# FoX's forget sums of the next head pair, issued from ScalarE's queue

## The chip, the cores and the metric

The kernel runs on 1 core of one Trainium2 chip. The metric is the device time of one execution in microseconds (us), as the median of several runs. The engines are named as in the profile: PE (TensorE's matmuls), PEld (its weight loads), DVE (VectorE), ACT (ScalarE), POOL (GpSimd), SP (SyncE, which here only issues DMAs). A q behind a name (SPq, ACTq) means that engine's sequencer: its queue, in which DMA issues and waits stand.

## The reference

One layer of a decoder trunk with 2048 tokens of 1024 channels in float32. What matters here is the forgetting attention (FoX) with 8 heads of 64 channels. Eight stick-breaking heads precede it, and the output projection, a gated MLP and a final norm follow it.

```
F = cumsum(log_f)                            # per head, over the 2048 tokens
s = q_blk . k * HEAD_DIM**-0.5               # one block of 128 queries
s = s + F_blk[..., None] - F[:, None, :]     # the forget sums
s = where(kpos <= qpos, s, -inf)
p = softmax(s)
out = p . v
```

F at the query's own position shifts a whole row and drops out of the softmax, so a kernel needs only F at the key positions, the same 2048 numbers for every query of a head.

## The kernel before

The attention runs over 32 units (kind, p, tb): first the stick-breaking heads ("sb"), then FoX ("fox"), each with four pairs p of heads, and for each pair four blocks tb of 512 queries. A unit handles two sub-blocks `j2` of 256 queries, and in each the two heads `hl` of the pair. The work grows with tb, since query block tb attends to all keys up to its own; the last block of a pair, tb = 3, is the longest, and the first block of the next pair, tb = 0, the shortest.

`fox_head` computes one head for 256 queries, as two rows of tiles (`qi`) of 128 queries. For each chunk of up to 512 keys, two matmuls (L596, L597) make the negated logits in PSUM; DVE (L675) adds the forget sums `Fb[ch]` and keeps the running minimum `mn`. For the chunk on the diagonal GpSimd (L672) first makes a masked copy `Fd` of the sums. ScalarE then takes the exponential of the whole row at once (L679), up to 2048 wide. After both rows, `weighted` transposes the probabilities on PE (L606), copies them out of PSUM as a high and a low half `at` (ScalarE L610, DVE L611) and multiplies them with V (L615).

`load_sums(p)` loads the forget sums of a pair: four tiles `Fb` of 128 x 1024 (512 KB each), for two heads and two halves of the keys, each a row of the DRAM tensor `fs` broadcast to all partitions (L653). They share four buffers (tag "xt"), so the next pair's sums can only be loaded when the old ones have been read for the last time, in unit tb = 3, `j2` = 1. `load_sums` is called at the start of unit tb = 0 of a pair (for pair 0 in unit 14, long before), and issues on SyncE's queue.

On the same queue go, among others, the loads of Q, K and V of the next unit (`load_unit`, L362 to L364), the loads `hp<-hs` of the projections' operands (`proj`, L468), those of the late modulation (`late_mod`, L776), `gate_m` (L796) and the stores of results. The projections of later units (`proj`, matmuls at L342 and L413) are interleaved with the attention: `follow` pulls them along by the goals of `pace`. What order the instructions take in each engine's queue is planned when the program is built, by a simulation of time; `tc.issue_after(ins)` forces what is written inside it to stand behind `ins` in the queue of that engine. The plan also lets every DMA, from whichever of the two queues, signal one of eight semaphores in turn.

Of the kernel before, what the change touches and what calls it, by code (L numbers as in the profile page):

```python
# [9 lines left out]
F32 = mybir.dt.float32  # L10
F32R = mybir.dt.float32r
BF16 = mybir.dt.bfloat16
AF = mybir.ActivationFunctionType
# [4 lines left out]
P = 128  # L18
S = 2048
D = 1024  # L20
# [4 lines left out]
TB = 512  # L25
NTB = S // TB
# [8 lines left out]
def kernel(ctx: ExitStack, tc: tile.TileContext, x, c, w_ada, b_ada, g_attn, w_in, b_fgate,  # L35
                      g_out_fox, g_out_sb, w_out, g_mlp, w_up, conv_w, conv_b, w_down, g_final, out):
    nc = tc.nc
# [30 lines left out]
    fs = dram.tile([NH, S], F32, name="fs")  # L68
# [56 lines left out]
    def open_pool(name, side=None, space=None):  # L125
        st = pools[name] = ExitStack()
        kw = dict(space=space) if space is not None else {}
        return st.enter_context(tc.tile_pool(name=name, bufs=1, side=side, reuse_waits="tile", **kw))
# [9 lines left out]
    px = open_pool("px", side="right")  # L138
    sm = open_pool("mod", side="right")

    def bank(pool, tag, bufs):
        return pool.tile([P, 512], F32, name=f"ps_{tag}", tag=tag, bufs=bufs)
# [74 lines left out]
    b = pv()  # L217
# [376 lines left out]
    def logits(cw, qcols, hl, Q, K):  # L594
        b = qk()
        nc.tensor.matmul(b[:, :cw], Q[:, hl, 0, qcols], K[:, hl, :cw], start=True, stop=False)  # L596
        marks.append(nc.tensor.matmul(b[:, :cw], Q[:, hl, 1, qcols], K[:, hl, :cw], start=False, stop=True).ins)  # L597
        return b
# [46 lines left out]
                         ch == n - 1 and m == 0, ch == 0 and m == nk - 2, kts[0] == 2 * j)  # L645
                yield

    def load_sums(p):
        sums = [[], []]
        for t in range(0, NTB, 2):  # L650
            for h in range(2):
                b = px.tile([P, D], F32, name="Fb", tag="xt", bufs=4)
                nc.sync.dma_start(b, fs[2 * p + h:2 * p + h + 1, t * TB:(t + 2) * TB].to_broadcast([P, D]))  # L653
                sums[h] += [b[:, 0:TB], b[:, TB:D]]
        return sums

    def fox_head(j, qc, hl, Q, K, V, o, Fb, ls):
        n = (2 * j + 2 + 3) // 4
        rows_ = []
        for qi in range(2):  # L660
            W = (2 * j + qi + 1) * P
            a = sx.tile([P, S], F32, name="p", bufs=4)
            mn = None
            for ch in range(n):
                need = min(512, W - ch * 512)
                b = logits(max(need, 2 * P), slice((qc + qi) * P, (qc + qi + 1) * P), hl, Q, K[ch])
                sl = slice(ch * 512, ch * 512 + need)
                m2 = sx.tile([P, 1], F32, name="mn", bufs=8)
                add = Fb[ch]
                if ch == n - 1:  # L670
                    add = px.tile([P, TB], F32, name="Fd", tag="hf_a", bufs=2)
                    mask[:] = [nc.gpsimd.affine_select(  # L672
                        out=add[:, :need], in_=Fb[ch][:, :need], pattern=[[-1, need]], base=need - P,
                        channel_multiplier=1, compare_op=ALU.is_ge, fill=BIG).ins]
                nc.vector.tensor_tensor_reduce(out=a[:, sl], in0=b[:, :need], in1=add[:, :need], scale=1.0,  # L675
                                               scalar=3e38 if mn is None else mn, op0=ALU.add, op1=ALU.min,
                                               accum_out=m2)
                mn = m2
            nc.scalar.activation(a[:, 0:W], a[:, 0:W], AF.Exp, scale=-1.0, bias=mn, accum_out=ls[:, hl, qc + qi:qc + qi + 1])  # L679
            rows_.append(a)  # L680
            yield
        for m in range(0, 2 * j + 2, 2):
            weighted(o, [m, m + 1], lambda kt, qi: rows_[qi][:, kt * P:(kt + 1) * P], V, hl, m == 0, m == 2 * j,
                     m == 2 * j)
            yield

    sums, step, mask = [], [], []
    deferred = []
    marks = []

    def tick(n=1):
# [5 lines left out]
    def attend(kind, p, tb, res, Fbs):  # L697
        Q = res[tb][0]
        K = [r[1] for r in res]
        V = [r[2] for r in res]  # L700
        oT = sb.tile([P, TB], F32, name="oT", bufs=2)
        last_unit = (kind, p, tb) == units[-1]
        if kind == "fox":
            ls = sx.tile([P, 2, 4], F32, name="ls", bufs=2)
        mp = p if kind == "fox" else p + 4

        def head_var(j2):
            sq = (sx.tile([P, 2 * P], F32, name="sq", bufs=1) if kind == "sb" and (p, tb) != (3, NTB - 1) else
                  px.tile([P, TB], F32, name="sq", tag="z", bufs=2)[:, 0:2 * P])
            cols_ = slice(j2 * 2 * P, (j2 + 1) * 2 * P)  # L710
            nc.gpsimd.tensor_mul(sq, oT[:, cols_], oT[:, cols_])

            def reduce():
                b = bank(psd, "t", 2) if last_unit and j2 else pt()
                for t in range(2):
                    nc.tensor.matmul(b[:, 2 * t:2 * t + 2], sq[:, t * P:(t + 1) * P], headsel, start=True, stop=True)
                v = var[tb][:, 2 * j2:2 * j2 + 2, 2 * mp:2 * mp + 2]
                bv = b[:, 0:4].rearrange("p (t h) -> p t h", t=2)
                if kind == "fox":
                    l = ls[:, :, 2 * j2:2 * j2 + 2]  # L720
                    nc.vector.scalar_tensor_tensor(l, l, EPS, l, ALU.mult, ALU.mult)
                    nc.vector.scalar_tensor_tensor(v, bv, 1.0 / HD, l.rearrange("p h t -> p t h"), ALU.mult, ALU.add)
                else:
                    nc.vector.tensor_scalar(v, bv, 1.0 / HD, EPS, ALU.mult, ALU.add)

            deferred.append([reduce, 13])

        for j2 in range(2):
            j = 2 * tb + j2
            for hl in range(2):  # L730
                o = bank(psc, "bc", 2) if (kind, p, tb) == units[-2] else pv()
                if kind == "sb":
                    yield from sb_head(j, 2 * j2, hl, Q, K, V, o)
                else:
                    yield from fox_head(j, 2 * j2, hl, Q, K, V, o, Fbs[hl], ls)
                o2 = sb.tile([HD, 2 * P], F32, name="o2", bufs=2)
                step[1] = nc.scalar.activation(o2, o[HD:P, 0:2 * P], AF.Copy).ins
                nc.vector.tensor_add(oT[hl * HD:(hl + 1) * HD, j2 * 2 * P:(j2 + 1) * 2 * P], o[0:HD, 0:2 * P], o2)
            head_var(j2)
        nc.sync.dma_start(os_[mp][tb], oT)  # L740
        yield
# [285 lines left out]
    Fbs = None  # L1027
    tail = None
    big = orp = None
    for i, u in enumerate(units):  # L1030
        kind, p, tb = u
        nxt = units[i + 1] if i + 1 < len(units) else None
        if u == ("sb", 1, 0):
            forget_sums()
            next(lm)
        if u == ("fox", 0, 0):
            close_pool("sx")
            sx = open_pool("fx", side="right")
        if i == 14 or (kind == "fox" and tb == 0 and p):
            Fbs = load_sums(p if kind == "fox" else 0)  # L1040
        n = attend_steps(u)
        if i >= len(units) - 2:
            head_root(i - len(units) + 2)
            head_scale(i - len(units) + 2, pt(), sx)
        if nxt is None:
            tail = first_out()
        if i == len(units) - 2:
            for _ in ahead:
                projected[0] += 1
            drain(lm)  # L1050
            close_pool("sl", "psa")
            psc = open_pool("psc", side="right", space=PSUM)
            big = open_pool("big")
            orp = open_pool("orp")
            tail = first_mix()
        goals = list(pace(i))

        def follow(m):
            while projected[0] < goals[min(m, n - 1)]:
                with tc.issue_after(marks[max(0, len(marks) - 1 - LAG)]) if START <= i < ENDQ else nullcontext():  # L1060
                    if next(ahead, 1) is not None:
                        break
            if nxt and projected[1] > i + 1 and loaded_units[0] == i + 1:
                loaded_units[0] += 1
                load_unit(*nxt, results[nxt[:2]])

        interleave(attend(kind, p, tb, results[kind, p], Fbs), n, [(lm if i >= LATE else None, PER, False), (tail, 17 + IDLE if nxt is None else 13, True)], follow)
        while nxt and loaded_units[0] == i + 1:
            next(ahead, None)
            follow(n)  # L1070
# [225 lines left out]
    for u in range(1, NU):  # L1296
        for c in range(8 if u == 1 else 0, 16):
            t, n, q = chunk(u, c)
# [148 lines left out]
    for sblk, order in enumerate(orders):  # L1447
# [47 lines left out]
        a, b = bank_a(), bank_a()  # L1495
# [32 lines left out]
    for kp in range(PRE):  # L1528
        if kp % 2 == 0:
            pre = ho.tile([P, 2, 2, TB], F32, name="pre", tag="xh", bufs=3)  # L1530
        t = pre[:, kp % 2]
# [153 lines left out]
    for i in range(7):  # L1685
        nxt = {}
        kept = []
        for s in range(2):
# [7 lines left out]
            for kp in range(NKP):  # L1696
                a = ahead_a.pop((i, s, kp), None)
                if a is None:
                    a = a_operand(i, s, kp, raw_a())
# [63 lines left out]
```

## Time and profile before

| What | Value |
|---|---|
| median of 3 runs | 2949.75 us (2949.39 to 2951.26) |
| the profiled execution's own time | 2943.39 us |
| its span | 2941.4 us |
| mean granted TensorE clock | 0.993 |
| busy: PE, PEld, DVE, ACT, POOL | 97%, 84%, 74%, 57%, 31% |
| DMA | 601.89 MB, mean 205 GB/s |
| loads of the forget sums (L653) | 16 of 512 KB, all on SyncE |

The span is the time from the first to the last instruction of the one profiled execution; the execution's own time is 2.0 us longer. Times in the views count from the span's start. In a timeline each row has start, duration, engine, line and tiles, and, in brackets, how long the engine sat idle before and who ended that. In a list of waits each row has who waited, for whom, the total, how often and the longest. In a table of stretches each row has the stretch, its length, the busy time and number of instructions of PE, PEld, DVE, ACT and POOL, the granted clock, the share of the DMA engines and GB/s.

### The profile page before, as it was taken

To read this page: it belongs to the slowest core of one execution; us is meant where nothing else is said; L and a number is where in the kernel's file an instruction comes from. 1 tells how busy PE (TensorE), PEld (TensorE's weight loads), DVE (VectorE), ACT (ScalarE), POOL (GpSimd) and SP (SyncE) were. 2 spreads that over 40 slices of the span, in tenths; PEclk is the share of its full clock that TensorE was granted. 3 is DMA by queue.
4 is the path that set the end of the run, shared out by engine and by line. 5 is a ranking of instruction groups with operands and counts; after the bars stand their busy time and mean duration, and the time that the engine had idled before them with its cause. 6 is when DMAs were issued, how large, how long until landed. Compare 5 with 4: busy or idle time off the path is not lost.

```text
span 2941.4 us, 45922 instructions
## 1 busy us (share of the span) xinstructions
PE 2867.8 (97%) x15772; PEld 2459.7 (84%) x15772; DVE 2179.5 (74%) x3464; ACT 1686.0 (57%) x3187; POOL 901.1 (31%) x967
## 2 busy tenths in 40 slices
PE   8999999999999999999999999999999999999998
PEld 7888888888988988888888788888788888888887
DVE  5787778877886656658843788888998888575476
ACT  5776767677776656658744554444444445433342
POOL 0431322243032423231213344444254543142200
PEclk8999999999999999999999999999999999999999
DMA  9749756867469794794537775554754444975644
GB/s 293 255 139 321 236 188 207 301 211 229 162 212 356 269 277 139 232 323 140 182 120 233 245 232 128 130 136 129 236 132 125 130 130 132 309 257 185 216 158 151
DMA packets 348346, 601.89 MB, mean 205 GB/s; under 512 B 34672, under 2 KB 178800, under 8 KB 348112
## 3 DMA queue, kind: packets, MB, share of 16 engines
q1 hardware_dynamic: 324208, 558.06, 57.7%
q0 software_dynamic: 10880, 20.97, 4.3%
q10 hardware_dynamic: 13024, 19.93, 1.9%
q8 instruction: 124, 2.03, 0.3%
q14 instruction: 110, 0.90, 0.1%
HBM read 420.77 MB, written 177.02 MB: 203 GB/s over the span
## 4 chain that ended last, share of the span: by engine, by line
PE 46%; DMA 3%; DVE 2%; SPq 1%; ACT 1%; issue 1%; POOL 0%; DVEq 0%; ACTq 0%; POOLq 0%
PE ps_o L1315 19%; PE ps_t L1315 7%; PE ps_o L1614 6%; PE ps_t L1614 3%; PE ps_bc L1614 3%; PE ps_o L912 1%; PE ps_pv L615 1%; DMA r<-rstd 1%; PE ps_bc L912 1%; PE ps_pt L606 1%; PE ps_o L1609 1%; DMA wo<-wos 1%; DMA hm<-hf_m 1%; SPq L895 1%; DVE op L46 1%
## 5 line engine op out<-in xcount | busy, mean ns | idle before, releaser
L1315 PE MATMUL ps_o<-op,wu 128*128 128x512 f32 x2592 | 608.0, 389 | 2.0 <-DVE snap L1366 1.5
L1315 PEld LDWEIGHTS ps_o<-op,wu 128*128 128x128 f32 x2592 | 486.2, 188 | 103.9 <-DVE snap L1366 1.9
L611 DVE TENSOR_TENSOR at<-ps_pt,at 128x512 fp32r<-128x512 f32 (+1 forms) x576 | 366.1, 652 | 100.2 <-ACT at L610 97.3
L636 DVE TENSOR_TENSOR_SCAN a<-r,a 128x512 f32<-128x512 f32 (+2 forms) x320 | 368.3, 1167 | 77.8 <-ACT a L631 39.9
L342 PE MATMUL ps_pj<-hp,w_qk 128*128 128x512 f32 x1512 | 411.2, 403 | 14.5 <-DMA hp<-hs 12.9
L610 ACT ACTIVATE at<-ps_pt 128x512 fp32r<-128x512 f32 (+1 forms) x576 | 318.5, 576 | 139.1 <-PE ps_pt L606 123.1
L615 PE MATMUL ps_pv<-at,V 128*128 128x256 f32 x2216 | 386.8, 292 | 9.3 <-DVE at L611 4.2
L615 PEld LDWEIGHTS ps_pv<-at,V 128*128 128x128 f32 x2216 | 320.9, 190 | 39.8 <-DVE at L611 11.4
L342 PEld LDWEIGHTS ps_pj<-hp,w_qk 128*128 128x128 f32 x1512 | 275.4, 190 | 71.0 <-DMA hp<-hs 16.2
L45 ACT ACTIVATE wu<-wuraw 128x512 fp32r<-128x512 f32 x204 | 128.9, 632 | 248.5 <-PE ps_o L1315 190.1
L596 PE MATMUL ps_qk<-K,Q 128*128 128x512 f32 (+2 forms) x640 | 265.7, 416 | 5.6 <-ACT a L631 3.3
L413 PE MATMUL ps_pj<-w_v,hp 128*128 128x256 f32 (+1 forms) x1536 | 236.6, 288 | 2.1 <-DVE hp L422 1.6
L597 PE MATMUL ps_qk<-K,Q 128*128 128x512 f32 (+2 forms) x640 | 235.7, 369 | 0.0
L1315 PE MATMUL ps_t<-op,wu 128*128 128x512 f32 x888 | 220.8, 390 | 1.0 <-DVE op L46 1.0
L413 PEld LDWEIGHTS ps_pj<-w_v,hp 128*128 128x128 f32 x1536 | 209.0, 189 | 10.9 <-DVE q L373 1.5
L630 ACT ACTIVATE r<-ps_qk 128x512 f32<-128x512 f32 (+2 forms) x320 | 173.1, 541 | 58.2 <-PE ps_qk L597 55.5
L46 DVE TENSOR_TENSOR wu<-wuraw,wu 128x512 fp32r<-128x512 f32 x204 | 189.6, 930 | 18.1 <-ACT wu L45 16.7
L1315 PEld LDWEIGHTS ps_t<-op,wu 128*128 128x128 f32 x888 | 166.4, 188 | 36.5 <-DVE op L46 1.8
L606 PE MATMUL ps_pt<-edge,a 128*128 128x128 f32 x1088 | 185.1, 274 | 8.4 <-DVE a L636 7.8
L1614 PE MATMUL ps_o<-op 128*128 128x512 f32 x840 | 191.5, 389 | 0.0
L1614 PEld LDWEIGHTS ps_o<-op 128*128 128x128 f32 x840 | 157.7, 188 | 32.7
L679 ACT ACTIVATE p<-p,mn 128x128 f32<-128x128 f32 (+15 forms) x128 | 153.9, 1203 | 53.3 <-DVE mn L675 52.2
(342 smaller groups left out, 5237.6 us busy)
## 6 DMA issues: line engine op xcount, KB each, us to landing
hp<-hs SPq DMA_DIRECT2D x224, 512.0 KB
wuraw<-in_w_up_dram SPq DMA_DIRECT2D x80, 512.0 KB
ra<-g SPq DMA_DIRECT2D x136, 256.0 KB
rb<-in_w_down_dram SPq DMA_DIRECT2D x108, 256.0 KB
g<-u SPq DMA_DIRECT2D x80, 256.0 KB
hs<-hp SPq DMA_DIRECT2D x32, 512.0 KB
hp<-in_w_ada_dram SPq DMA_DIRECT2D x32, 512.0 KB
qk_fox<-q SPq DMA_DIRECT2D x32, 512.0 KB
```

Source lines behind the costliest of these rows:

```text
L46: (lo_engine or nc.gpsimd).tensor_sub(lo, src, f(hi))
L342: nc.tensor.matmul(acc, w[kt][:, a, n], h[:, bb], start=kt == 0 and i == 0, stop=kt == KT - 1 and i == 2)
L413: nc.tensor.matmul(av[:, t * width:(t + 1) * width], hts[kt][:, a, tok], w[1][kt][:, bb, 0:width], start=kt == 0 and m == 0, stop=kt == KT ...
L596: nc.tensor.matmul(b[:, :cw], Q[:, hl, 0, qcols], K[:, hl, :cw], start=True, stop=False)
L597: marks.append(nc.tensor.matmul(b[:, :cw], Q[:, hl, 1, qcols], K[:, hl, :cw], start=False, stop=True).ins)
L606: nc.tensor.transpose(b[:, i * P:(i + 1) * P], blk(kts[kk], qi), ident)
L610: copies = [nc.scalar.activation(at[:, 0, lo:], b[:, lo:], AF.Copy).ins, nc.vector.tensor_sub(at[:, 1, lo:], b[:, lo:], f(at[:, 0, lo:])).ins]
L611: nc.vector.tensor_sub(at[:, 1, lo:], b[:, lo:], f(at[:, 0, lo:])).ins]
L615: m = nc.tensor.matmul(o[:, 0:2 * P], V[kt // 4][:, kt % 4, hl, :], rhs, start=first and kk == 0 and w == 0, stop=last and kk == 1 and w == 1)
L636: nc.vector.tensor_tensor_scan(rev, r[:, 0:need][:, ::-1], rev, 0.0 if right[qi] is None else right[qi][:, 0:1], ALU.mult, ALU.add)
L1315: nc.tensor.matmul(b, w[:, p, j], o[:, q], start=first and i == 0, stop=last and i == 2, skip_group_check=True)
L1614: nc.tensor.matmul(b, a[:, p, t * P:(t + 1) * P], w[:, q], start=first and i == 0, stop=last and i == 2, skip_group_check=True)
```

## The change

`load_sums` now loads one head's two tiles, on a queue that it is given. For pairs 1 to 3 it is no longer called at the start of the pair. Instead it is called from within `fox_head` of the pair before, in unit tb = 3, `j2` = 1: once for each head, behind the exponential of the head's last row, on ScalarE's queue. Pair 0's sums stay in unit 14 on SyncE, now head by head.

```diff
-    def load_sums(p):
-        sums = [[], []]
+    def load_sums(p, hl, queue=nc.sync):
+        sums = []
         for t in range(0, NTB, 2):
-            for h in range(2):
-                b = px.tile([P, D], F32, name="Fb", tag="xt", bufs=4)
-                nc.sync.dma_start(b, fs[2 * p + h:2 * p + h + 1, t * TB:(t + 2) * TB].to_broadcast([P, D]))
-                sums[h] += [b[:, 0:TB], b[:, TB:D]]
+            b = px.tile([P, D], F32, name="Fb", tag="xt", bufs=4)
+            queue.dma_start(b, fs[2 * p + hl:2 * p + hl + 1, t * TB:(t + 2) * TB].to_broadcast([P, D]))
+            sums += [b[:, 0:TB], b[:, TB:D]]
         return sums
...
-            nc.scalar.activation(a[:, 0:W], a[:, 0:W], AF.Exp, scale=-1.0, bias=mn, accum_out=ls[:, hl, qc + qi:qc + qi + 1])
+            e = nc.scalar.activation(a[:, 0:W], a[:, 0:W], AF.Exp, scale=-1.0, bias=mn,
+                                     accum_out=ls[:, hl, qc + qi:qc + qi + 1])
+            if qi and then is not None:
+                with tc.issue_after(e.ins):
+                    then()
...
-                    yield from fox_head(j, 2 * j2, hl, Q, K, V, o, Fbs[hl], ls)
+                    then = None
+                    if j2 and tb == NTB - 1 and p < 3:
+                        then = lambda hl=hl: sums_of.setdefault(p + 1, []).append(load_sums(p + 1, hl, nc.scalar))
+                    yield from fox_head(j, 2 * j2, hl, Q, K, V, o, Fbs[hl], ls, then)
...
-        if i == 14 or (kind == "fox" and tb == 0 and p):
-            Fbs = load_sums(p if kind == "fox" else 0)
+        if i == 14:
+            sums_of[0] = [load_sums(0, hl) for hl in range(2)]
+        if kind == "fox" and tb == 0:
+            Fbs = sums_of[p]
```

More of the change, by code (lines that the diff above doesn't have):

```diff
@@ L646, in sb_head, with fox_head @@
                 yield
-    def load_sums(p):
-        sums = [[], []]
+    def load_sums(p, hl, queue=nc.sync):
+        sums = []
         for t in range(0, NTB, 2):
-            for h in range(2):
-                b = px.tile([P, D], F32, name="Fb", tag="xt", bufs=4)
-                nc.sync.dma_start(b, fs[2 * p + h:2 * p + h + 1, t * TB:(t + 2) * TB].to_broadcast([P, D]))
-                sums[h] += [b[:, 0:TB], b[:, TB:D]]
+            b = px.tile([P, D], F32, name="Fb", tag="xt", bufs=4)
+            queue.dma_start(b, fs[2 * p + hl:2 * p + hl + 1, t * TB:(t + 2) * TB].to_broadcast([P, D]))
+            sums += [b[:, 0:TB], b[:, TB:D]]
         return sums
-    def fox_head(j, qc, hl, Q, K, V, o, Fb, ls):
+    def fox_head(j, qc, hl, Q, K, V, o, Fb, ls, then):
         n = (2 * j + 2 + 3) // 4
@@ L688 @@
     deferred = []
+    sums_of = {}
     marks = []
```

## The prediction

> **What bounds the kernel now.** I read the page first, then the table of busy time by stretch over the attention of the FoX heads (870 to 1530 us), then the waits of SyncE's queue, and last the timelines of PE, SyncE and ScalarE at the three places where one head pair follows another.
>
> ```profile
> span 2941.4 us, 45922 instructions
> ...
> PE 2867.8 (97%) x15772; PEld 2459.7 (84%) x15772; DVE 2179.5 (74%) x3464; ACT 1686.0 (57%) x3187; POOL 901.1 (31%) x967
> ```
>
> PE is busy for 97% of the span. An edit that touches only SyncE's and ScalarE's queues can therefore win only where PE stands still because of them. The columns of the next table are: the stretch, its length, the busy time of the five engines, the granted clock, the share of the DMA engines and the rate.
>
> ```profile
> 1010.00:1060.00 50.00, 43.99 (x293) 39.88 (x292) 25.66 (x67) 29.73 (x61) 15.97 (x21) 0.93 0.94 269
> 1060.00:1180.00 120.00, 119.22 (x828) 109.07 (x827) 80.01 (x210) 76.81 (x147) 36.77 (x49) 1.00 0.55 185
> 1180.00:1220.00 40.00, 36.60 (x250) 33.30 (x249) 29.39 (x72) 27.23 (x56) 8.93 (x15) 0.91 0.67 207
> 1220.00:1350.00 130.00, 129.32 (x827) 114.79 (x826) 81.38 (x213) 83.09 (x152) 41.77 (x50) 1.00 0.77 261
> 1350.00:1390.00 40.00, 39.28 (x287) 35.09 (x285) 35.06 (x98) 33.76 (x75) 8.52 (x18) 1.00 0.73 218
> ```
>
> The pair changes lie in the first, third and fifth row. PE lacks 6.0 us in the first and 3.4 us in the third, and the granted clock is below 1.00 there; the fifth lacks only 0.7 us. The stretches between lack less than 1 us each. PE's timeline names the cause of both holes:
>
> ```profile
> 1052.80 2.93 PE L342 MATMUL ps_pj<-hp,w_qk 128*128 128x512 f32 x6 [6.01 <-DMA hp<-hs]
> ...
> 1208.81 2.93 PE L342 MATMUL ps_pj<-hp,w_qk 128*128 128x512 f32 x6 [3.40 <-DMA hp<-hs]
> ```
>
> Both times a projection matmul waits for its operand `hp`. Each hole also costs clock afterwards (third column from the end):
>
> ```profile
> 1053.00:1058.00 5.00, 5.00 (x16) 4.22 (x17) 0.20 (x1) 0.87 (x2) 0.00 (x0) 0.51 1.05 279
> ...
> 1209.00:1216.00 7.00, 7.00 (x29) 6.29 (x30) 2.65 (x6) 4.76 (x14) 2.52 (x4) 0.58 0.74 287
> ```
>
> PE is busy in all of these 5.00 and 7.00 us at clocks of 0.51 and 0.58, which loses 5.00 x 0.49 = 2.5 us and 7.00 x 0.42 = 2.9 us. The two holes thus cost 6.0 + 2.5 = 8.5 us and 3.4 + 2.9 = 6.3 us, together 14.8 us, 0.5% of the span. That is all there is to win nearby.
>
> **What SyncE's queue does there.** Its wait for the old sums to be read is long:
>
> ```profile
> SPq L653 <- DVE mn L675: 31.9, 7, 13.6
> ...
> 1167.74 0.34 SPq L740 DMA_DIRECT2D os<-oT  x1
> 1181.77 1.72 SPq L653 DMA_DIRECT2D Fb<-fs  x2
> 1189.81 3.01 SPq L363 DMA_DIRECT2D K<-qk_fox  x5
> 1192.92 0.53 SPq L653 DMA_DIRECT2D Fb<-fs  x1
> ...
> 1194.69 0.52 SPq L653 DMA_DIRECT2D Fb<-fs  x1
> ...
> 1200.74 0.33 SPq L468 DMA_DIRECT2D hp<-hs  x1
> ...
> SPq L363 <- PE ps_pt L606: 6.7, 1, 6.7
> ```
>
> For 13.6 us before 1181.77 the queue's head is the first load of the next pair. What stands behind it, though, is the K loads, and after the sums these wait another 6.7 us for PE themselves, until 1189.81. So the 13.6 us hold nothing up. The `hp` load that PE lacks from 1205.41 (1208.81 - 3.40) is issued at 1200.74 and PE starts at 1208.81, 8.1 us later. On a quieter stretch the same load took 1155.19 - 1151.16 = 4.0 us:
>
> ```profile
> 1151.16 0.34 SPq L468 DMA_DIRECT2D hp<-hs  x1
> ...
> 1155.19 1.66 PE L342 MATMUL ps_pj<-hp,w_qk 128*128 128x512 f32 x6 [0.47 <-DMA hp<-hs]
> ...
> 1192.00:1209.00 17.00, 13.60 (x107) 12.47 (x106) 12.65 (x32) 10.72 (x22) 2.17 (x5) 0.97 0.98 276
> 1028.00:1053.00 25.00, 18.99 (x134) 17.25 (x134) 12.04 (x33) 14.58 (x33) 5.80 (x9) 0.96 1.04 286
> ...
> SPq L364 <- DMA Fb<-fs: 2.2, 1, 2.2
> SPq L468 <- DMA Q<-qk_fox: 1.2, 1, 1.2
> ```
>
> In front of both holes the DMA engines are full (0.98 for 17 us, 1.04 for 25 us). The last two rows, from SyncE's waits between 1189 and 1205 us, show more: a load is not issued before an earlier, unrelated transfer has landed. The number of transfers in flight is limited.
>
> **The change, part by part.** *Sixteen loads leave SyncE's order or change it.* The four of pair 0 stay on SyncE at their place, in another order. They run during the stick-breaking attention that comes before, which covers them, so I cost them at nothing; without that cover it would be a wait like the 4.0 us above for one load. Twelve loads of 512 KB move to ScalarE, four at each pair change. The bytes stay.
>
> *ScalarE's part.* Issuing one DMA in its queue has a price in the stage behind attention:
>
> ```profile
> 1526.15 0.40 ACTq L1013 DMA_DIRECT2D hm<-hf_m  x1
> 1526.66 0.42 ACT L45 ACTIVATE mix<-r 128x256 fp32r<-128x256 f32 x1 [0.55 <-ACT hf_m L1011]
> ...
> 1366.60 0.19 ACT L679 ACTIVATION_READ_ACCUMULATOR p<-p,mn 128x1 f32 x1
> ...
> 1369.61 1.25 PE L606 MATMUL ps_pt<-edge,p 128*128 128x128 f32 x8 [0.43 <-DVE at L611]
> ```
>
> The engine idles 0.55 us for one issue, so 1.1 us for the pair behind each exponential and 6.6 us for all twelve. Queued behind are the mask copy, the `at` copies (L610) and the exponentials of the next unit; DVE's `at` subtraction and then PE wait for these. At pairs 0 to 1 and 1 to 2 the delay, at most 2.2 us for both heads, ends in the holes of 6.01 and 3.40 us, in which PE waits for a DMA anyway: 0 us, and 1.1 us for each head if a hole is gone. At pairs 2 to 3 there is no such hole; PE already waits 0.43 us for `at` some 3 us behind the end of the second head's exponential (1366.60 + 0.19). Bounds there: 0 (PE has other work queued) and 2.2 us (both heads on the path). I take 1.5: the second head whole, a third of the first.
>
> *SyncE's part.* Two issues of 0.53 and 0.52 us no longer stand ahead of the `hp` load of 1200.74. If nothing else holds it, it goes 1.1 us earlier. The lower bound is larger: if `hp` passed the whole megabyte of the second head's sums (1.05 MB at the stretch's 276 GB/s are 3.8 us), the hole of 3.40 us and its 2.9 us of clock would go, -6.3 us. The upper bound has the opposite sign, and needs the time at which the last exponential ends and who reads the new sums:
>
> ```profile
> 1033.52 0.18 ACT L679 ACTIVATION_READ_ACCUMULATOR p<-p,mn 128x1 f32 x1
> ...
> 1029.71 0.33 SPq L653 DMA_DIRECT2D Fb<-fs  x1
> ...
> 1035.27 0.51 SPq L653 DMA_DIRECT2D Fb<-fs  x1
> ...
> 1197.37 0.19 ACT L679 ACTIVATION_READ_ACCUMULATOR p<-p,mn 128x1 f32 x1
> ...
> 1197.85 0.75 POOL L672 TENSOR_SCALAR_AFFINE_SELECT Fd<-Fb 128x128 f32<-128x128 f32 x2 [2.06 <-DVE mn L675]
> ...
> 1205.77 0.28 DVE L675 CUSTOM_DVE_ANT_0 p<-ps_qk,Fd 128x128 f32<-128x128 f32 x1
> ```
>
> The sums were issued at 1192.92 and 1194.69; behind the exponential they go only from about 1197.6 (1197.37 + 0.19), so their 3.8 us of transfer may fall wholly into the time in which `hp` moves: +3.8 us. I take -0.5 us, near zero, because the engines are at 0.98 and the bytes ahead of or beside `hp` are the same. At pairs 0 to 1 I take 0: the second head's sums go at about 1033.7 in place of 1029.71 and 1035.27, and the DMA engines are full for 25 us on end, so the last of the same bytes lands at the same time.
>
> This row of 0.98 bears on a rule. The Trainium skill (DMA: Bandwidth & Descriptors, Issuing engines are not separate DMA queues) says that DMAs started by different engines end on the same 16 DMA engines and interleave, so that another issuing engine saves only the sequencer's issue time. By that rule the change is worth no more than the issue time, and the trace, with one queue's work filling the engines, does not contradict it.
>
> *The later reading of the sums.* With 4.0 to 8.1 us from issue to use, the second head's sums are there at 1201.6 to 1205.7. GpSimd's mask read its first ones at 1197.85, but DVE used the mask only at 1205.77, so this costs between 0 and the masks' own 0.75 us; I take 0, the landing in the middle of its range.
>
> Sum: 1.5 - 0.5 = +1.0 us on the profiled execution's 2943.4 us (2941.4 us of span and 2.0 around it), 2944.4 us. The median of the runs, 2949.75, stands 6.4 us higher, so the forecast is 2950.8 us. A difference under about 0.2%, 5.9 us, is what a measurement of this kernel can hardly tell from none.
>
> **The rivals.** *Faster: the `hp` loads come in time.* The build plans the order of each queue anew, and with the sums off SyncE both `hp` loads may be placed and land earlier. For it: both holes end with `hp`, and SyncE is slowed by the sums' landing (2.2 us above). Against it: full DMA engines. The second hole gone: 2949.75 - 6.3 = 2943.5 us; both gone: 2949.75 - 14.8 = 2935.0 us. A shorter hole might keep the clock. The Trainium skill (TensorE: Matmul & The Clock Gate, Part 1: The HAM clock gate) states that the clock halves after an idle window of some 3.4 us. The hole of 3.40 us did cost clock here, so by trace and rule alike a gain of 1.1 us there would be worth up to 1.1 + 2.9 = 4.0 us.
>
> *Slower: ScalarE is held in front of its loads.* ScalarE's loads may need an earlier transfer's landing as SyncE's do. SyncE waited up to 2.2 us for one. For a pair of loads that is up to 4.4 us, and with the issue 5.5 us, in which no `at` copy and no exponential leaves ScalarE. It decides wherever SyncE's transfers are many when the exponential ends, which is so behind the second head at every pair change. At pairs 2 to 3 all of 5.5 us is exposed; at 1 to 2 the hole covers 3.4 of it, leaving 2.1, and `hp` may come 3.8 us later; at 0 to 1 the 6.01 us cover it. Together 11.4 us: 2961.2 us; the first alone: 2955.3 us.
>
> *No change in effect.* The planned order may put the loads so late or the neighbours so alike that the DMA engines see the same stream; the time is then 2949.75 us.
>
> **How the numbers follow.** The forecast has 0.40, no effect 0.05, the faster rival 0.27 and the slower 0.28. The two unlike signs are nearly equal because one new hole costs what an old one does (6.3 to 8.5 us), and a new plan can open as well as close one. That gives faster by over 0.2% 0.27, within 0.2% 0.45, slower 0.28. The forecast's own range is 2944 to 2956. For eight in ten it reaches from 2937, between one hole and both gone, to 2961, where ScalarE is held as above.
>
> **What would show it.** Right: PE's holes of 6.01 and 3.40 us stand with a like size, behind `hp`; ScalarE's DMA rows show four loads at each pair change, some 0.53 us of idle each; the DMA engines stay near 1.0 before the holes. The faster rival: no hole over 2 us in these stretches and a clock of 1.00. The slower: ScalarE idle for over 2 us behind a 2048-wide exponential, with PE idle soon after `at`. I am wrong if the difference comes from stretches outside the three pair changes, which would mean that a new order of the whole attention decides, not these loads.

## The result and the profile after

| | median | range | runs |
|---|---|---|---|
| before, beside it | 2948.99 us | 2945.04 to 2956.83 | 19 |
| after | 2956.68 us | 2947.92 to 2968.25 | 19 |

The ratio after to before is 1.0025, with a 95% interval of 1.0017 to 1.0033: the changed kernel is slower by 7.7 us. The profiled execution of after took 2962.53 us, 5.9 us above its own median, while that of before lay 5.6 us below the median of 2948.99. So the 19.1 us between the two profiles are mostly scatter (6.7 us of them arise before the FoX attention begins, ahead of the first moved load), and the traces are compared stage by stage below, not by their totals.

The change was carried out as described. These rows are from the view of the tile `Fb` in the profile of after: twelve of the loads are now issued by ScalarE's queue, and four by SyncE's. The last row is from the list of what GpSimd waited for in front of its masks (total us, times).

```profile
L652 ACTq DMA_DIRECT2D Fb<-fs x12: 326/334/445, 1020.9 to 1370.9; - x12
L652 SPq DMA_DIRECT2D Fb<-fs x4: 319/400/498, 539.9 to 555.1; - x4
...
  DMA Fb<-fs: 26.3, 3
```

The three pair changes look as before. The table of stretches of after, at the places that answer to those shown of before:

```profile
1012.00:1046.00 34.00, 32.80 (x228) 29.70 (x228) 19.63 (x51) 21.88 (x38) 15.47 (x17) 1.00 0.73 223
1046.00:1066.00 20.00, 14.96 (x96) 13.25 (x95) 8.92 (x23) 10.55 (x27) 3.25 (x8) 0.91 1.03 305
1190.00:1222.00 32.00, 28.66 (x203) 26.16 (x202) 23.98 (x60) 23.81 (x48) 5.08 (x11) 0.95 0.72 230
1357.00:1397.00 40.00, 39.10 (x285) 34.81 (x284) 34.88 (x97) 33.20 (x73) 8.53 (x19) 1.00 0.74 218
...
1060.00:1064.00 4.00, 3.56 (x13) 2.88 (x13) 0.00 (x0) 0.00 (x0) 0.00 (x0) 0.57 1.04 357
1216.00:1222.00 6.00, 5.52 (x25) 4.93 (x26) 2.03 (x5) 3.56 (x8) 1.43 (x3) 0.72 0.74 276
```

PE's timeline of after names the same cause for the missing time:

```profile
1060.44 2.93 PE L342 MATMUL ps_pj<-hp,w_qk 128*128 128x512 f32 x6 [5.04 <-DMA hp<-hs]
...
1216.48 2.33 PE L342 MATMUL ps_pj<-hp,w_qk 128*128 128x512 f32 x6 [3.34 <-DMA hp<-hs]
```

Both holes stand (6.01 and 3.40 us before), both end with `hp`, the DMA engines are full in front of the first (1.03), and the clock falls behind both. At pairs 2 to 3 PE lacks 0.9 us of 40.

A new hole is 900 us further on, in the MLP, at the place where the first half of the sequence gives way to the second. PE's timeline and two stretches of after:

```profile
2128.56 0.39 PE L1324 MATMUL ps_o<-op,wu 128*128 128x512 f32 x1
2133.05 6.83 PE L1324 MATMUL ps_o<-op,wu 128*128 128x512 f32 x17 [4.10 <-DVE op L46]
```

```profile
2129.00:2133.00 4.00, 0.00 (x0) 0.00 (x0) 3.97 (x5) 0.57 (x1) 2.77 (x2) 0.87 0.61 178
2132.00:2139.00 7.00, 5.95 (x14) 4.67 (x15) 3.49 (x6) 1.26 (x2) 2.68 (x3) 0.51 0.97 332
```

The same place in the profile of before, in PE's timeline and in the table of stretches:

```profile
2118.41 0.73 PE L1315 MATMUL ps_t<-op,wu 128*128 128x512 f32 x2 [0.95 <-DVE op L46]
2119.62 6.88 PE L1315 MATMUL ps_o<-op,wu 128*128 128x512 f32 x29 [0.47 <-DVE op L46]
```

```profile
2119.00:2126.00 7.00, 6.53 (x29) 5.29 (x29) 4.45 (x7) 1.26 (x2) 2.24 (x2) 1.00 0.90 310
```

After has one wait of 4.10 us and then a clock of 0.51; before has two waits of 0.95 and 0.47 us, and a clock of 1.00. PE waits for `op`, the operand of the MLP's products, which DVE makes. DVE's timeline of after shows what it did first:

```profile
2127.39 1.67 DVE L1407 SCALAR_TENSOR_TENSOR u<-u 64x512 f32<-64x512 f32 x1
2128.98 1.75 DVE L1408 TENSOR_TENSOR u<-u 64x512 f32<-64x512 f32 x1
2130.76 1.64 DVE L1207 TENSOR_TENSOR tt<-xh 128x512 f32<-128x512 f32 x1
2132.32 0.68 DVE L46 TENSOR_TENSOR op<-xh,op 128x512 fp32r<-128x512 f32 x1
```

The two gating products of the first half's rest (`gate`, L1407 and L1408) stand ahead of `tt` (L1207) and of the `op` (L46) for which PE waits. The profile of before has them in the other order: `tt` and `op` first, then the gating (there L1398 and L1399).

```profile
2118.28 0.68 DVE L1198 TENSOR_TENSOR tt<-xh 128x512 f32<-128x512 f32 x1
2118.89 0.68 DVE L46 TENSOR_TENSOR op<-xh,op 128x512 fp32r<-128x512 f32 x1
2119.60 0.69 DVE L1398 SCALAR_TENSOR_TENSOR u<-u 64x512 f32<-64x512 f32 x1
2120.21 0.69 DVE L1399 TENSOR_TENSOR u<-u 64x512 f32<-64x512 f32 x1
```

Nothing in the diff touches these lines. The order of every queue is planned when the program is built, and the loads at the change from pair 1 to pair 2 shift that plan a little from there on. In the two traces the instructions of PE, DVE, GpSimd and SyncE follow in the same order again behind the attention, except here: between 2087 and 2175 us of before, around the change of halves, all four differ. Below, "the new order" and "the old order" mean this piece of the MLP alone.

### The profile page after: what moved, and what is told of

It is laid out like the page before. It is cut to its first block, busy times and chain, and to the rows that moved or that the text cites. A ratio compares the mean times of both kernels' runs of the same rounds, so it can differ in the third digit from the quotient of the medians.

```text
span 2960.6 us, 45916 instructions
## 1 busy us (share of the span) xinstructions
PE 2876.0 (97%) x15772; PEld 2462.9 (83%) x15772; DVE 2176.5 (74%) x3464; ACT 1689.5 (57%) x3187; POOL 903.6 (31%) x967
## 4 chain that ended last, share of the span: by engine, by line
PE 75%; DMA 13%; DVE 4%; ACT 3%; issue 2%; POOL 2%; SPq 1%; POOLq 0%; ACTq 0%; DVEq 0%
PE ps_o L1324 20%; PE ps_pj L342 8%; PE ps_t L1324 8%; PE ps_pv L615 6%; PE ps_o L1623 5%; PE ps_pt L606 5%; PE ps_pj L413 5%; PE ps_o L919 3%; PE ps_qk L596 3%; PE ps_qk L597 3%; PE ps_t L1623 2%; PE ps_bc L1623 2%; DMA hp<-hs 2%; DMA hp<-in_w_ada_dram 1%; DMA vd<-xt 1%
## 5 line engine op out<-in xcount | busy, mean ns | idle before, releaser
L615 PE MATMUL ps_pv<-at,V 128*128 128x256 f32 x2216 | 386.6, 292 | 11.4 <-DVE at L611 4.7
L413 PEld LDWEIGHTS ps_pj<-w_v,hp 128*128 128x128 f32 x1536 | 210.6, 190 | 10.6 <-DVE q L373 1.6
L46 DVE TENSOR_TENSOR wu<-wuraw,wu 128x512 fp32r<-128x512 f32 x204 | 188.5, 924 | 18.3 <-ACT wu L45 17.2
```

What stands on the lines that cost most here:

```text
L46: (lo_engine or nc.gpsimd).tensor_sub(lo, src, f(hi))
L413: nc.tensor.matmul(av[:, t * width:(t + 1) * width], hts[kt][:, a, tok], w[1][kt][:, bb, 0:width], start=kt == 0 and m == 0, stop=kt == KT ...
L615: m = nc.tensor.matmul(o[:, 0:2 * P], V[kt // 4][:, kt % 4, hl, :], rhs, start=first and kk == 0 and w == 0, stop=last and kk == 1 and w == 1)
```

## The experiments

Two theories were set against each other. *The order:* the cost is the new order of the MLP, and the loads cost nothing. *The loads:* the cost comes from where the loads of the sums are issued. Whole runs of one kernel scatter by 3 to 5 us (standard deviation), as much as the effect, so each run is read twice: by its time beside before on the same chip, and by its trace. For the latter the last two columns take the time at which PE starts its 5,500th, 9,500th, 12,000th and 12,500th matmul; the attention of the FoX heads lies between the first two (626.0 us in the profile of before), the change of halves between the last two (118.0 us). Each shows the difference from the profile of before. The ratio is formed from all the runs and not from the two medians: the +6.0 us of e3_middle would be 1.0020, its ratio is 1.0012, some 3.5 us.

| kernel | sums of pairs 1, 2, 3 | MLP | median minus before's, us | ratio (95%) | FoX attention | change of halves |
|---|---|---|---|---|---|---|
| after | all moved | new | +7.7 | 1.0025 (1.0017 to 1.0033) | -0.3 | +5.1 |
| e1_again | all moved | new | +1.2 | 1.0012 (1.0000 to 1.0024) | -1.1 | +3.1 |
| e7_third | all moved | new | +6.9 | 1.0021 (1.0009 to 1.0034) | +1.6 | +2.3 |
| e11_fourth | all moved | new | +4.0 | 1.0018 (1.0006 to 1.0030) | -1.7 | +2.2 |
| e3_middle | 2 moved | new | +6.0 | 1.0012 (1.0000 to 1.0024) | 0.0 | +2.3 |
| e5_flip | as before | new | +7.0 | 1.0021 (1.0009 to 1.0032) | -0.8 | +2.6 |
| e8_unread | not loaded | new | +5.4 | 1.0013 (1.0002 to 1.0025) | -0.4 | +5.0 |
| e2_outer | 1 and 3 moved | old | +1.8 | 1.0005 (0.9994 to 1.0015) | -1.1 | -0.8 |
| e4_one_matmul | all moved | old | +3.4 | 1.0007 (0.9996 to 1.0019) | +4.3 | -0.9 |
| e10_order_again | all moved | old | +2.6 | 1.0008 (0.9997 to 1.0020) | -0.5 | 0.0 |
| e6_control | as before | old | +2.6 | 1.0000 (0.9987 to 1.0013) | -0.5 | -0.8 |
| e9_unread_order | not loaded | old | +1.0 | 1.0004 (0.9992 to 1.0016) | +0.2 | -0.8 |

### The changed kernel again: e1_again, e7_third, e11_fourth

No edit. Expected of the first:

> The changed kernel once more, for its time beside the others and for a second profile. Theory P (the plan): the loads themselves cost about nothing, and the time comes from the order that the build plans anew for the MLP around 2100 us, where the first profile had a hole of 4.10 us and 6.8 us at half clock: +4 to +9 us against before, and the hole stands again, over 3 us with a dip of the clock. Theory L (the loads): they delay ScalarE and GpSimd's masks at the three pair changes: +4 to +9 us as well, but the hole near 2130 us comes and goes from profile to profile.

Expected of the second and third:

> The changed kernel once more. If the order of the MLP is its cost, a hole of over 2 us near 2130 us again and a stage there 3 to 5 us longer than in the kernel before, and a time 2 to 7 us above that of the kernel before. If the hole was an accident of single executions, it is absent here. Both holes of PE behind hp at the first two pair changes, 3 to 7 us each, stand by either theory.

> The changed kernel a fourth time, as the measure for the run before it. By the theory of the order: a hole of over 3 us near 2130 us with half clock behind it, and 3 to 7 us above the kernel before. By the theory that the loads cost it: 3 to 7 us too, and the kernel with the idle matmul equal to it.

Measured: +1.2, +6.9 and +4.0 us. The hole near 2130 us is there each time, 3.62, 3.47 and 3.27 us long. It is a property of the kernel, not of one execution. The +1.2 us of e1_again lie below the 4 to 9 us that both theories expected, and the change of halves took 2.3 us more in e7_third where 3 to 5 were expected. The size of the whole loss varies more than the hole does; what that variation goes with is shown below.

### One part of the change: e2_outer, e3_middle

```diff
-                    if j2 and tb == NTB - 1 and p < 3:
+                    if j2 and tb == NTB - 1 and p in (0, 2):     # e3_middle: p in (1,)
...
+        if kind == "fox" and tb == 0 and p and p - 1 not in (0, 2):     # e3_middle: (1,)
+            sums_of[p] = load_both(p)      # as before, on SyncE
```

Pair 0's sums are loaded by `load_both` as well, in the order of heads that they have in before.

> Only the sums of pairs 1 and 3 are loaded from ScalarE's queue; pair 2's stay on SyncE at their old place. In this version the planned order of PE, DVE and ScalarE is that of the kernel before but for the loads. Theory P: 0 us, at most 2 us either way. Theory L: two thirds of the change's cost, +5 us (at least +3).

> Only the sums of pair 2 are loaded from ScalarE's queue. This version has the changed kernel's new order of the attention from about 1210 us and of the MLP around 2100 us. Theory P: the whole cost, +5 to +9 us. Theory L: one third of it, +2.5 us.

Measured: +1.8 and +6.0 us by the medians, with ratios whose intervals overlap (by its ratio e3_middle is nearer to the 2.5 us of the theory of the loads), so the times alone don't part the two. The traces do. Moving the loads of pair 2 alone gives the new order and a hole of 3.32 us; moving the eight others leaves the old order and no such hole. Eight of twelve moved loads are thus in the kernel without the loss in the MLP.

### The changed kernel with the old order: e4_one_matmul, e10_order_again

```diff
+    nudge = bank(psd, "t", 2)
+    for _ in range(1):
+        nc.tensor.matmul(nudge[:, 0:2 * P], ones, edge[:, 0:2 * P], start=True, stop=True)
     close_pool("orp")
```

One idle matmul ahead of the MLP is enough to make the plan come out in the old order. All twelve loads stay on ScalarE.

> The changed kernel with one more matmul of 256 columns (about 0.1 us), whose result nobody reads, ahead of the MLP. With it the build plans the MLP in the order of the kernel before (but for a rotation of PSUM banks), while the attention keeps the changed kernel's order and all its loads. Theory P: 0 us against before, within 2 us, and no hole over 2 us near 2130 us. Theory L, and a theory A that the new order of the attention costs the time: +5 to +9 us as the changed kernel.

> The changed kernel with one idle matmul ahead of the MLP again, now beside a run of the changed kernel on the same chip. If the order of the MLP is the change's cost: no hole over 2 us near 2130 us, a time 3 to 5 us below that of the changed kernel beside it, and within 2 us of the kernel before. If the moved loads cost it: as the changed kernel, within 1.5 us.

Measured: +3.4 and +2.6 us, both above the 2 us at most that the theory of the order expected, and e10_order_again 1.4 us under the changed kernel beside it where that theory said 3 to 5. The times are inconclusive again; the trace is not. PE's matmuls of this line between 2118 and 2140 us, of e4_one_matmul (idle time before them and its cause at the end):

```profile
L1327 PE MATMUL ps_o<-op,wu 128*128 128x512 f32 x60 | 15.1, 393 | 1.3 <-DMA wu<-wus 1.3
```

The same of after:

```profile
L1324 PE MATMUL ps_o<-op,wu 128*128 128x512 f32 x45 | 14.1, 462 | 4.1 <-DVE op L46 4.1
```

The wait for `op` is gone, and the mean matmul took 393 ns where it takes 462 ns in after, with its lower clock.

### The old place with the new order: e5_flip, e6_control

```diff
         n = attend_steps(u)
+        if i == 28:
+            nudge = pt()
+            for _ in range(4):       # e6_control: 2
+                nc.tensor.matmul(nudge[:, 0:2 * P], ones, edge[:, 0:2 * P], start=True, stop=True)
```

This goes into the kernel before. Four idle matmuls give the new order, two leave the old one.

> The kernel before, with the sums' loads where they were, and four idle matmuls of 128x256 (of the tile of ones and a mask, whose result nobody reads) added to the queue in the last unit of the first half of the FoX projections' work, unit 28. Four matmuls are worth well under 1 us by themselves, but the plan then puts the MLP's instructions around the change of its two halves in the order that they have in the changed kernel. If that order of the MLP costs the time, PE has a hole of over 2 us near 2130 us, with half clock behind it, and the stage from about 2071 to 2189 us is 3 to 5 us longer than in the kernel before (ratio about 1.0012). If the moved loads cost it, that stage is as in the kernel before within 1 us and the time is 2949.7 us within 1.5.

> The same with two idle matmuls in place of four: the MLP keeps the order of the kernel before. By both theories no hole over 2 us near 2130 us, the stage there within 1 us of the kernel before, and the time 2949.7 us within 1.5. A longer time here would mean that the idle matmuls, and not the order, cost something in the kernel with four.

Measured: +7.0 us (ratio 1.0021) and +2.6 us (ratio 1.0000). The kernel with its sums untouched and the new order is as slow as the changed kernel on the same chip (2955.27 and 2955.08 us). The same group of matmuls in both, e5_flip first:

```profile
L1319 PE MATMUL ps_o<-op,wu 128*128 128x512 f32 x46 | 13.5, 433 | 3.5 <-DVE op L46 3.5
```

```profile
L1319 PE MATMUL ps_o<-op,wu 128*128 128x512 f32 x70 | 16.9, 393 | 1.4 <-DMA wu<-wus 1.4
```

This is the clearest pair: the loss is here without any moved load. Its size at the change of halves, 2.6 us, is a little under the 3 to 5 expected. DVE's timeline of e6_control shows too that long gating products alone make no hole; they took as long there as in after, but behind the `op`:

```profile
2116.77 0.68 DVE L1202 TENSOR_TENSOR tt<-xh 128x512 f32<-128x512 f32 x1
2117.38 0.68 DVE L46 TENSOR_TENSOR op<-xh,op 128x512 fp32r<-128x512 f32 x1
2118.09 1.67 DVE L1402 SCALAR_TENSOR_TENSOR u<-u 64x512 f32<-64x512 f32 x1
2119.68 1.77 DVE L1403 TENSOR_TENSOR u<-u 64x512 f32<-64x512 f32 x1
```

### No loads at all: e8_unread, e9_unread_order

```diff
-        if i == 14 or (kind == "fox" and tb == 0 and p):
+        if i == 14:
             Fbs = load_sums(p if kind == "fox" else 0)
```

These two leave out the loads of the sums of pairs 1 to 3, so all pairs use pair 0's sums. In e9_unread_order two idle matmuls in unit 28 are added as above, which gives the old order.

> The kernel before without any load of the forget sums of pairs 1 to 3: all four pairs use pair 0's sums. 6.3 MB of transfers and twelve DMA issues at the pair changes are gone. If the sums' bytes or issues in front of hp make PE's holes at the first two pair changes, each is shorter by 2 to 4 us and the time lower by 5 to 12 us. If hp is late for other reasons, the holes stand within 1.5 us. The MLP has the order of the changed kernel here: by the theory of the order the hole of over 2 us near 2130 us is there, though no sums are loaded from any queue; by the theory of the loads it is not.

> As the kernel that loads no forget sums for pairs 1 to 3 (all use pair 0's sums), with two idle matmuls of 128x256 in unit 28, with which the MLP has the order of the kernel before. The order of the attention is planned anew either way. If the order of the MLP is what costs time, no hole over 2 us near 2130 us, and about 4 us less than the same kernel with the other order of the MLP, whose ratio was 1.0013: some 2949 us, no cost left against the kernel before, and a gain of at most 5 us, since the holes behind hp were 2.72 and 2.95 us without any load. If the attention's new order or the absence of the loads made that ratio, the time stays at 2953 us.

Measured: +5.4 and +1.0 us. With the new order even a kernel without these loads loses, and with the old one it gains nothing. The first hole behind `hp` shrinks, the second hardly; e8_unread's timeline of PE:

```profile
1054.32 2.56 PE L342 MATMUL ps_pj<-hp,w_qk 128*128 128x512 f32 x6 [2.72 <-DMA hp<-hs]
...
1211.88 2.93 PE L342 MATMUL ps_pj<-hp,w_qk 128*128 128x512 f32 x6 [2.95 <-DMA hp<-hs]
```

In e9_unread_order they are 4.25 and 2.73 us. The expected 2 to 4 us less came at the first hole in e8_unread (2.72 us against 6.01) but not in e9_unread_order; in the eleven kernels with these loads this hole is 4.1 to 7.0 us long. At the second hole it did not come (3.40 us before, 2.9 to 4.6 in nine of the ten other kernels with these loads, 1.90 in e11_fourth). So the sums' bytes may be a part of what makes `hp` late at the first hole, and are not what makes it late at the second. The FoX attention as a whole took -0.4 and +0.2 us against before: even without the loads nothing of the 14.8 us was won.

### What the runs say together

At the change of halves the seven kernels with the new order need 2.2 to 5.1 us more than before (mean 3.2), the five with the old order -0.9 to 0.0 (mean -0.7); no kernel is in between. The means of the medians, +5.4 and +2.3 us, differ by about as much, 3.2 us, and the means of the ratios, 1.0017 and 1.0005, by 3.7 us. By both, the order makes about half of the 7.7 us. Within the old order, kernels with moved loads stand at +1.8, +3.4 and +2.6 us and those without at +2.6 and +1.0: what the moved loads cost by themselves, some 0.8 us by these means, was not told from zero. Why all five stand 1 to 3 us above before by their medians, though each interval holds 1.0, stays open.

Much of the scatter goes with the granted clock. Among the runs of each kernel the slower ones have the lower mean clock (correlation -0.53 to -0.82): the changed kernel's 2968.25 us came with 0.987, its 2947.92 us with 0.991. It arises where nothing was changed, too. Up to 1010 us all kernels have the same order, apart from pair 0's four loads; yet eleven of the twelve need 5.5 to 11.1 us more than the profile of before up to PE's 5,500th matmul, and only e6_control, with +0.2 us, does not. The profile of before is a lucky one there.

In the output projection, where after shows +4.2 us, the kernels with the new order stand at -1.1 to +4.9 us (mean 2.5) and those with the old order at -2.0 to +1.9 (mean 0.1). PE waits there for DVE near 1650 us in all of them; the clock fell to a half around it in six kernels with the new order, in one with the old, and not in before. Whether the order has a part in that or chance alone stays open. The 3.4 us near 2800 us show in no other kernel.

No version here beats the kernel before, and none of the experiments points to one: what is left to win is behind `hp`, and leaving these loads out did not win it.

## Why the prediction was right, and where it was wrong

The time, 2956.7 us, lies in the range given for eight in ten (2937 to 2961), 0.7 us above the forecast's own (2944 to 2956), and the reason for expecting little from the loads held. But the loss of 7.7 us, 0.25%, is not the forecast's +1.0: "slower by over 0.2%" had 0.28, and the part of the loss that the runs trace is none of the forecast's terms. That the range holds the time is to that extent luck. By the steps:

- *The holes behind `hp` stand.* Right: 5.04 and 3.34 us in after, 4.3 and 3.5, 4.2 and 4.6, 6.6 and 1.9 in its three other profiles. Letting the edit win none of it was right, and e8_unread shows that taking the loads away would not have won it either.
- *SyncE's 13.6 us wait held nothing up.* Right. In after SyncE's K load waits 22.1 us for PE's transposes at that place, in the list of waits below; the wait has changed its owner.

```profile
SPq L363 <- PE ps_pt L606: 22.1, 1, 22.1
```

  The `hp` load, in SyncE's timeline of after:

```profile
1205.88 0.70 SPq L468 DMA_DIRECT2D hp<-hs  x1
```

  It did go earlier: 7.3 us before PE stopped (1216.48 - 3.34 = 1213.14), where in before it was 4.7 us (1200.74 and 1205.41). It was 6.7 to 7.8 us in the seven kernels with pair 2's sums on ScalarE, and 4.7 to 5.6 us in the four that load them on SyncE. But PE started on it 10.6 us after the issue in place of 8.1, with the DMA engines at 0.96 in between, so the hole kept its length. The term of 1.1 us was real as an issue and worth nothing as an arrival.
- *0.55 us for each issue on ScalarE, 1.5 us in all at pairs 2 to 3.* Wrong in size; measured 0. In ScalarE's timeline of after the issues (ACTq) lie within the exponential's own time or just ahead of it, and the next copy starts without idle time:

```profile
1202.52 2.00 ACT L678 ACTIVATE p<-p,mn 128x2048 f32<-128x2048 f32 x1
1202.70 0.81 ACTq L652 DMA_DIRECT2D Fb<-fs  x2
1204.41 0.19 ACT L678 ACTIVATION_READ_ACCUMULATOR p<-p,mn 128x1 f32 x1
1204.51 0.41 ACT L609 ACTIVATE at<-edge 128x256 fp32r<-128x256 f32 x1
...
1370.05 0.33 ACTq L652 DMA_DIRECT2D Fb<-fs  x1
1370.50 2.00 ACT L678 ACTIVATE p<-p,mn 128x2048 f32<-128x2048 f32 x1
1370.88 0.45 ACTq L652 DMA_DIRECT2D Fb<-fs  x1
1372.40 0.19 ACT L678 ACTIVATION_READ_ACCUMULATOR p<-p,mn 128x1 f32 x1
1372.49 0.41 ACT L609 ACTIVATE at<-edge 128x256 fp32r<-128x256 f32 x1
```

  The row from which the 0.55 us came had an issue that sends the result of the activation just ahead of it (`hf_m`, which the row names): it had to wait for that activation's end, and the engine behind it. The loads of the sums need nothing of the exponential, and here the queue issued them ahead of the engine. The Trainium skill (Perfetto Trace Analysis, Per-instruction lifecycle) describes this: the sequencer hands an activation to a wait queue and takes its next instruction. The trace agrees, and with it "behind the exponential" means behind its hand-over: the loads of 1202.70 were issued 0.18 us into it, and that of 1370.05 0.45 us before it began.
- *ScalarE held in front of its loads* (the slower rival). Its mechanism is real, at pairs 0 to 1:

```profile
1041.27 0.19 ACT L678 ACTIVATION_READ_ACCUMULATOR p<-p,mn 128x1 f32 x1
1043.05 1.01 ACTq L652 DMA_DIRECT2D Fb<-fs  x2
1044.16 0.42 ACT L609 ACTIVATE at<-edge 128x256 fp32r<-128x256 f32 x1 [2.70 <-DMA K<-qk_fox]
```

  In before the copy followed the exponential at once. Here ScalarE stood still for 2.70 us, by the profile until a K load had landed (2.6 to 2.9 us in the six other kernels that move pair 1's sums; two of these profiles name PE's transposes instead of the K load). As the prediction said for this pair, the hole covers it. At the two other pair changes it didn't occur. The rival's price of 5.5 to 11.4 us was therefore not paid, although the measured loss is near it: a time that fits a rival is no evidence for it.
- *SyncE's part of -0.5 us* (bounds -6.3 to +3.8) *and the sums read later, 0 us.* GpSimd's masks now wait 26.3 us for the sums, 9.8, 9.4 and 7.1 us at the three pair changes, which looks dear. PE hardly feels it: the whole FoX attention took -0.3, -1.1, +1.6 and -1.7 us against before in the four profiles of the changed kernel, and +4.3 and -0.5 us in e4_one_matmul and e10_order_again, which have the same attention; on average +0.4 us. The forecast for it was +1.0, which this scatter doesn't tell from 0.
- *The Trainium skill's rule (DMA: Bandwidth & Descriptors, Issuing engines are not separate DMA queues) that another issuing engine saves only the issue time.* The trace agrees: with the loads on ScalarE the stage gained nothing that was told from zero.
- *The step that failed* is the sum's scope. It ended with the attention, and counted every later stage at nothing without naming a reason. The front part says that each queue's order is planned when the program is built; the prediction used this for the `hp` loads in its faster rival and for "a new order of the whole attention" in its last sentence. By that sentence the prediction is wrong in its mechanism, since the traced difference comes from outside the pair changes; and the sentence was itself only half right, for the attention's new order cost nothing that was told from zero, and two DVE instructions of the MLP, 900 us on, cost 2 to 5 us. From the profile of before the risk could be seen, if not its sign: PE waited there for `op` twice already, 0.95 and 0.47 us, with no reserve.

## What to carry to other kernels

Where the order of the queues is planned as a whole, an edit is costed in two parts: what it does at its place, and a lottery over every stage planned after it; the places where PE waits already by a little, with DVE in front, are where that lottery pays out. Before an effect of a few tenths of a per cent is put down to an edit, bring about the same order without the edit, and the edit without that order: some idle matmuls did both here. A DMA issue behind a long activation cost its engine nothing here, unless it had to wait for a landing or for that activation's own result. And a load that is issued earlier while the DMA engines are full need not arrive earlier.

## What the runs showed of the hardware

**DVE beside GpSimd.** The gating and `tt` took 1.64 to 1.75 us in after and 0.68 to 0.69 us in before, with the same shapes. In after GpSimd ran elementwise operations all that time:

```profile
2126.18 2.33 POOL L1246 TENSOR_TENSOR ws<-wuraw 128x512 f32<-128x512 f32 x1 [1.78 <-DMA wuraw<-in_w_up_dram]
2128.58 1.59 POOL L1247 TENSOR_TENSOR wuraw<-wuraw 128x512 f32<-128x512 f32 x1
2130.26 1.59 POOL L1248 TENSOR_TENSOR ws<-wuraw 128x512 f32<-128x512 f32 x1
```

In before GpSimd's run of three ended at 2117.82, just ahead of these operations. By these durations some 3 us of the hole's 4.10 us are this lengthening (an estimate: 5.06 us for the three against 2.06), which the new order puts in front of the `op`. The Trainium skill (GPSIMD Engine Reference, Specifications) states that GpSimd's SBUF interfaces are shared with VectorE, with contention for DVE instructions that have two SBUF inputs; the rows agree, with a factor of 2.4 for them. But it isn't always DVE that is held up. In e6_control `tt` and `op` (2116.77 and 2117.38) kept 0.68 us, and GpSimd's operation beside them took 4.76 us, where the same one took 1.29 us at 2124.61:

```profile
2114.45 4.76 POOL L1241 TENSOR_TENSOR ws<-wuraw 128x512 f32<-128x512 f32 x1 [4.16 <-DMA wuraw<-in_w_up_dram]
```

**The clock after short holes.** A hole of 2.72 us cost clock (e8_unread), one of 2.92 us did not (e2_outer), nor did one of 1.90 us (e11_fourth). The table of stretches, in that order:

```profile
1054.30:1058.00 3.70, 3.68 (x13) 3.14 (x14) 0.00 (x0) 0.42 (x1) 0.00 (x0) 0.56 1.04 378
```

```profile
1214.00:1224.00 10.00, 7.08 (x50) 6.63 (x50) 5.17 (x15) 6.55 (x19) 4.54 (x6) 1.00 0.89 327
```

```profile
1216.70:1220.00 3.30, 3.22 (x18) 2.82 (x19) 1.15 (x2) 2.13 (x5) 0.55 (x1) 1.00 0.93 364
```

The prediction weighed the Trainium skill's window of some 3.4 us (TensorE: Matmul & The Clock Gate, Part 1: The HAM clock gate). As a bound on the hole it does not hold here, since 2.72 us sufficed; that the window runs freely, which the same section says, fits that a longer hole was spared. The clock records of the traces show it: in all thirteen the clock changes only at points of a grid of 3.41 us, which lies differently in every execution. The 2.72 us of e8_unread (1051.61 to 1054.32) filled 80% of one piece of the grid, 1051.37 to 1054.78, and the next piece ran at 0.50. The 2.92 us of e2_outer (1214.10 to 1217.02) were cut by a grid point at 1215.52 into 1.4 and 1.5 us, and cost no clock. At the change of halves the half clock lasted 6.83 us in after and e8_unread (+5.1 and +5.0 us) and 3.41 us in the five others with the new order (+2.2 to +3.1).
